# Attention: two rows of one PSUM tile take mask, maxima and exponentials as a pair; reciprocals copied ahead of the lower part; a second bank for the late gates

## The chip, the core and the metric

The kernel runs on one core of one Trainium2 chip. The metric is the device time of one execution in microseconds (us). Each kernel is timed in several runs, and the median is compared. The profile is of one more execution, taken by the hardware profiler.

## What is computed

The reference is one block of a hybrid model, on 1024 tokens of width 1024, in float32: a projection of the normed input, an attention branch with forget gates (8 heads of 64), a recurrent branch (8 heads), sigmoid gates that merge the two, and a convolutional feed-forward part. The change concerns the attention branch and the gates:

```python
logits = einsum('bhqd,bhkd->bhqk', q[q0:q1], k[:q1]) * scale + cum[q] - cum[k]
logits = where(causal, logits, -inf)
probs  = softmax(logits, axis=-1)
o      = einsum('bhqk,bhkd->bhqd', probs, v[:q1])
...
gate_fox, gate_rwkv = split(sigmoid(p_gate), 2)
merged = gate_fox * (o_fox @ fox_w_out) + gate_rwkv * (o_rwkv @ rwkv_w_out)
```

## The kernel before

Matrix products are made in three passes of float32r: each operand is split into a high part (a rounding copy on ACT, named `..._hi`, `th`) and a low part (a subtraction on DVE, `..._lo`, `tl`), and hi*hi + hi*lo + lo*hi are added up in PSUM.

**Stages.** First the input projections with the recurrent branch beside them, then the attention stage, then the branch stage (`br`, the products with `w_br`, multiplied by the gates into `mg`), then the output projection and the feed-forward part. The change lies in the attention stage.

**The attention stage.** For each of 8 heads the queries are cut into 8 rows of 128 (i = 0 to 7), taken in pairs I = 3, 0, 2, 1 (for the last head 0, 1, 3, 2). Three chains are interleaved:

- `s_chain` makes the logits of a row in PSUM (`lg`): 128 x 128(i+1). There are two such tiles of two banks each. A row with i > 3 has a tile to itself; rows 0 and 1 share one, and so do rows 2 and 3, each in its own bank. Then `softmax` is started (L1144): DVE adds the causal mask to the last 128 columns (L1146) and takes the negated maximum `nm` (L1147), ACT makes the exponential `P` with its row sum (L1156). After the exponential of the last row in it, the PSUM tile is free for other logits.
- `t_chain` turns P by transposes on TensorE into a PSUM tile `tp`; `halve` (L1213) splits it: ACT copies `th` (L1215), DVE subtracts `tl` (L1220). At the end of each half of the queries (rows 4 to 7, then 0 to 3) of the heads 0 to 6 the reciprocals of four row sums are transposed into the same tile `tp`, and `spread` (L1172) copies them out (`rt`, on ACT, L1175), stores them to DRAM (`d_rs`, L1177) and loads them back spread over the partitions (`R`, L1181), both by ACT's DMA queue. `rt` has one buffer.
- `a_chain` multiplies th and tl with the values into `ov` (half of a PSUM bank); `collect` copies it out, and POOL multiplies by R.

**What sets the order.** PE, DVE and ACT run in the order in which the program is written here. A small planner, `Weave`, writes it: each chain yields the time at which it is next due, by a cost that the code states for each operation (`weave.use("DVE", ..., 310 + 1.04 * n)`); where no chain is due, it fills TensorE with matmuls of the next projection. In the attention stage the fill is the last 7 gate projections, as 14 halves of 24 matmuls (`late_gate`, L1280), all into one PSUM bank `rk_ps`. When a half is done, ACT applies tanh (`gs`, L1295), and only then can the next half write the bank; `weave.hold` tells the planner for how long it may not fill. What is left of the fill behind the last `ov` runs before the branch stage. The order after that stage's start on ACT, DVE, POOL and SP is set by the compiler's scheduler.

## Time and profile before

| | us |
|---|---|
| median of 3 runs | 1659.14 (1657.43 to 1660.03) |
| the profiled execution, its own time | 1663.44 |
| its span, first to last instruction | 1661.7 |
| TensorE busy in it | 1621.0 (98%) |
| the granted TensorE clock, mean | 0.991 |
| first logits, last `ov`, first branch matmul | 619.2, 812.53 (its end), 826.57 |

A profile row of an instruction reads: start, duration, engine, line, operation, output<-input, shapes, and in brackets how long the engine had been idle and what it waited for. `PE` is TensorE, `PEld` its weight load, `SPq` and `ACTq` are DMA issues. Times in these rows are us from the start of the span.

### The profile page before, as it was taken

What the parts mean: (1) busy time and instruction counts of PE and PEld (TensorE: products, weight loads), DVE (VectorE), ACT (ScalarE), POOL (GpSimd) and SP (SyncE); (2) the same over time, 40 slices, a digit from 0 to 9 for tenths busy, and PEclk for the clock granted to TensorE, in tenths of its full rate; (3) what the DMA queues carried; (4) which work ended last, traced back from release to release, by engine and by line L of the source; (5) the groups of instructions that cost most, each with busy time, mean ns of one, the idle gap of its engine ahead of it and who ended that gap; (6) DMA issues with size and microseconds to landing.
All of it is one profiled execution on the core that took longest, in us unless ns stands there. A gap on an engine that the chain in (4) does not pass through costs nothing.

```text
span 1661.7 us, 25960 instructions
## 1 busy us (share of the span) xinstructions
PE 1621.0 (98%) x9756; PEld 1329.5 (80%) x9756; DVE 1202.9 (72%) x2350; ACT 809.2 (49%) x1473; POOL 136.6 (8%) x169
## 2 busy tenths in 40 slices
PE   7999999999999998999999999999999999999998
PEld 5777877887877777887788888888888888888886
DVE  6875877887886536866579445897777777786677
ACT  7663434443446556665513144654444444555455
POOL 0010101211101020222022000000000000000000
PEclk8999999999999999999999999999999999999999
DMA  9587644443433246542487310243223223574463
GB/s 347 191 308 221 159 131 127 131 125 91 116 101 87 92 156 136 152 119 84 143 284 270 146 73 36 70 138 104 95 96 120 96 95 108 202 272 153 127 209 108
DMA packets 123902, 241.72 MB, mean 145 GB/s; under 512 B 39816, under 2 KB 48320, under 8 KB 123776
## 3 DMA queue, kind: packets, MB, share of 16 engines
q1 hardware_dynamic: 114944, 220.94, 41.1%
q0 software_dynamic: 7600, 17.25, 3.8%
q10 hardware_dynamic: 1232, 1.86, 0.4%
q8 instruction: 77, 1.26, 0.3%
q14 instruction: 49, 0.40, 0.1%
HBM read 174.43 MB, written 65.56 MB: 144 GB/s over the span
## 4 chain that ended last, share of the span: by engine, by line
PE 82%; DVE 8%; ACT 4%; DMA 3%; issue 2%; SPq 0%; POOL 0%; ACTq 0%; DVEq 0%; POOLq 0%
PE X L144 13%; PE D L144 13%; PE Y L144 6%; PE gt L144 6%; PE ps_rkv L144 5%; PE wo L144 5%; PE br L144 5%; PE W L144 3%; PE rk_ps L144 3%; PE qk L144 3%; PE v L144 3%; PE low L144 1%; PE lg L144 1%; PE ov L144 1%; PE sp L144 1%
## 5 line engine op out<-in xcount | busy, mean ns | idle before, releaser
L144 PE MATMUL D<-op,op 128*128 128x512 f32 x924 | 209.8, 390 | 0.0
L144 PEld LDWEIGHTS D<-op,op 128*128 128x128 f32 x924 | 173.4, 188 | 36.2 <-DVE op L1372 0.3
L144 PE MATMUL X<-T_m,S 128*128 128x512 f32 x440 | 107.3, 390 | 0.1
L144 PEld LDWEIGHTS X<-T_m,S 128*128 128x128 f32 x440 | 82.5, 188 | 18.2 <-ACT T_m L1797 0.6
L1371 ACT CAST op<-g 128x512 fp32r<-128x512 f32 x77 | 47.8, 621 | 72.1 <-PE D L144 48.2
L1372 DVE TENSOR_TENSOR op<-g,op 128x512 fp32r<-128x512 f32 x77 | 53.0, 689 | 40.9 <-ACT op L1371 40.8
L1608 DVE SCALAR_TENSOR_TENSOR c<-ab,vec,c 128x512 f32<-128x512 f32 x88 | 65.9, 750 | 19.5 <-ACT c L1611 17.9
L1220 DVE TENSOR_TENSOR tl<-tp,th 128x512 fp32r<-128x512 f32 (+1 forms) x80 | 50.3, 633 | 29.0 <-ACT th L1215 28.4
L1572 DVE TENSOR_TENSOR S<-ur,S 128x512 fp32r<-128x512 f32 x66 | 45.5, 691 | 35.6 <-ACT S L1568 35.4
L270 DVE TENSOR_TENSOR lo_in<-raw_in,hi_in 128x512 fp32r<-128x512 f32 x84 | 58.0, 729 | 16.4 <-PE gt L144 7.5
L1568 ACT CAST S<-ur 128x512 fp32r<-128x512 f32 x66 | 41.0, 622 | 55.6 <-DVE ur L1561 30.6
L1572 DVE TENSOR_TENSOR A<-ur,A 128x512 fp32r<-128x512 f32 x64 | 44.1, 689 | 30.9 <-ACT A L1568 30.7
L266 ACT CAST hi_in<-raw_in 128x1024 fp32r<-128x1024 f32 x42 | 43.9, 1048 | 46.1 <-PE ps_rkv L144 26.2
L795 DVE TENSOR_TENSOR t<-E,M 128x60 f32<-128x60 f32 (+24 forms) x248 | 55.0, 222 | 11.9 <-DMA M<-sm 5.9
L144 PE MATMUL Y<-T_h,A 128*128 128x512 f32 x264 | 63.5, 390 | 0.0
L144 PE MATMUL Y<-T_h,S 128*128 128x512 f32 x264 | 63.3, 390 | 0.0
L799 DVE TENSOR_TENSOR E<-E,t 128x60 f32<-128x60 f32 (+24 forms) x248 | 56.9, 230 | 5.8
L144 PE MATMUL X<-B_b,A 128*128 128x512 f32 x252 | 60.8, 390 | 0.0
L144 PE MATMUL W<-B_f,A 128*128 128x512 f32 x252 | 60.6, 390 | 0.0
L1156 ACT ACTIVATE P<-lg,nm 128x896 f32<-128x896 f32 (+3 forms) x64 | 47.4, 743 | 24.4 <-DVE nm L1147 21.2
L144 PEld LDWEIGHTS Y<-T_h,A 128*128 128x128 f32 x264 | 49.6, 188 | 10.3
L144 PEld LDWEIGHTS Y<-T_h,S 128*128 128x128 f32 x264 | 49.6, 188 | 10.3
(493 smaller groups left out, 4076.9 us busy)
## 6 DMA issues: line engine op xcount, KB each, us to landing
raw_in<-in_w_in SPq DMA_DIRECT2D x50, 512.0 KB
wm<-in_w_mod SPq DMA_DIRECT2D x48, 512.0 KB
ur<-in_w_up SPq DMA_DIRECT2D x44, 512.0 KB
g<-d_g SPq DMA_DIRECT2D x35, 512.0 KB
d_g<-gs SPq DMA_DIRECT2D x44, 256.0 KB
d_g<-c SPq DMA_DIRECT2D x33, 256.0 KB
d_st<-qh SPq DMA_DIRECT2D x64, 128.0 KB
d_gate<-gs SPq DMA_DIRECT2D x32, 256.0 KB
```

The lines of the kernel that those rows point to most:

```text
L144: weave.last = nc.tensor.matmul(o, lhsT, rhs, start=start, stop=stop, skip_group_check=more)
L266: i = nc.scalar.copy(hi, raw)
L270: nc.vector.tensor_tensor(lo[:, c : c + NH], raw[:, c : c + NH], f32(hi[:, c : c + NH]), op=ALU.subtract)
L795: i = tt(tv, E32[:, 0:J, s : s + 1].to_broadcast([128, J, W]), M32[:, s : s + 1, s + 1 : 32].to_broadcast([128, J, W]), op=ALU.mult)
L799: tt(E32[:, 0:J, s + 1 : 32], E32[:, 0:J, s + 1 : 32], tv, op=ALU.add)
L1156: nc.scalar.activation(e[:, 0:n], lg[:, 0:n], AF.Exp, bias=nm[:, 0:1], accum_out=total)
L1220: tt(tl[:, 0:w], tp[:, 0:w], f32(th[:, 0:w]), op=ALU.subtract)
L1371: nc.scalar.copy(hi, src)
L1372: tt(lo, src, f32(hi), op=ALU.subtract)
L1568: nc.scalar.copy(hi, src)
L1572: tt(lo, src, f32(hi), op=ALU.subtract)
L1608: stt(c, ab[:, x + hf * NH : x + hf * NH + NH], V("conv_w", 22 * x + i), c, op0=ALU.mult, op1=ALU.add)
```

## The change

`softmax` now takes a tuple of rows. The two rows that share a PSUM tile are started together when the second one's logits are issued: one mask over both blocks, two maxima, then two exponentials one behind the other. In the last head the scaling of P goes to a function of its own, `scaled`. In `halve` the copy of the reciprocals is issued right behind `th`, ahead of `tl`; its DMA is due 300 ns later by the planner's clock. A late gate that begins when `weave.late` is 2 (behind the attention chains) would take the bank of `ov` in turn with `rk_ps`.

```diff
@@ -1110,7 +1110,8 @@
         seq = [(h, I) for h in range(8) for I in ((0, 1, 3, 2) if h == 7 else (3, 0, 2, 1))]
         lg_free, tp_free, pl_free, ps_free, th_free, ov_free = (deque([0.0] * n) for n in (2, 2, 4, 2, 3, 1))
         probs, av_queue, halves, sums, norms, inverse, landed = {}, deque(), {}, {}, {}, {}, set()
-        ov_ps = pb.tile([128, NH], F32, tag="big", name="ov")[:, 0:256]
+        ov_bank = pb.tile([128, NH], F32, tag="big", name="ov")
+        ov_ps = ov_bank[:, 0:256]
         rk_ps = pb.tile([128, NH], F32, tag="big", name="rk_ps")
 
         def slot(free):
@@ -1138,42 +1139,64 @@
                         c1 = min(n, c0 + NH)
                         mm(lg[:, c0:c1], qa[:, qs], ka[:, c0:c1], start=True, stop=False)
                         mm(lg[:, c0:c1], qb[0:68, qs], kb[0:68, c0:c1], start=False, stop=True)
-                    weave.spawn(softmax(h, i, n, lg), 351)
+                    if i > 3:
+                        weave.spawn(softmax(h, (i,), lgt), 351)
+                    elif i % 2:
+                        weave.spawn(softmax(h, (i - 1, i), lgt), 351)
                     yield 0
 
-        def softmax(h, i, n, lg):
-            nm = at.tile([128, 3], F32, tag="nm", name=f"nm{h}_{i}", bufs=4)
-            tt(lg[:, n - 128 : n], lg[:, n - 128 : n], f32(tri_r), op=ALU.add)
-            nc.vector.tensor_reduce(nm[:, 0:1], lg[:, 0:n], axis=AX.X, op=ALU.max, negate=True)
-            yield weave.use("DVE", weave.now, 310 + 1.04 * n) + 140 - weave.now
-            e = (at.tile([128, S], F32, tag="P", name=f"P{h}_{i}", bufs=4) if i > 3 else
-                 at.tile([128, NH], F32, tag="Ps", name=f"P{h}_{i}", bufs=2))
-            p, hf = h // 2, i // 4
-            if (h, hf) not in sums:
-                sums[h, hf] = at.tile([128, 8], F32, tag="sums", name=f"sums{h}_{hf}", bufs=4), []
-            sm, done = sums[h, hf]
-            total = nm[:, 1:2] if h == 7 else sm[:, i % 4 : i % 4 + 1]
-            nc.scalar.activation(e[:, 0:n], lg[:, 0:n], AF.Exp, bias=nm[:, 0:1], accum_out=total)
-            t = weave.use("ACT", weave.now, 250 + 0.83 * n)
-            if i > 3 or i % 2:
-                lg_free.append(t + 210)
-            if h == 7:
-                yield t + 140 - weave.now
-                nc.vector.reciprocal(nm[:, 2:3], total)
-                ts(e[:, 0:n], e[:, 0:n], nm[:, 2:3], None, op0=ALU.mult)
-                t = weave.use("DVE", weave.now, 230 + 0.53 * n)
-            probs[h, i] = t + 210, e
-            done.append(i)
+        def softmax(h, rows, lgt):
+            hf, k = rows[0] // 4, len(rows)
+            d = rows[0] * 128
+            if k == 1:
+                tt(lgt[:, d : d + 128], lgt[:, d : d + 128], f32(tri_r), op=ALU.add)
+            else:
+                m = lgt[:, d : d + 768].rearrange("p (a c) -> p a c", c=128)[:, ::5, :]
+                tt(m, m, f32(tri_r).unsqueeze(1).to_broadcast([128, 2, 128]), op=ALU.add)
+            t = weave.use("DVE", weave.now, 190 + 130 * k)
+            part = []
+            for i in rows:
+                n = (i + 1) * 128
+                nm = at.tile([128, 3], F32, tag="nm", name=f"nm{h}_{i}", bufs=4)
+                lg = lgt[:, i % 2 * NH :] if k > 1 else lgt
+                nc.vector.tensor_reduce(nm[:, 0:1], lg[:, 0:n], axis=AX.X, op=ALU.max, negate=True)
+                t = weave.use("DVE", weave.now, 120 + 1.04 * n)
+                part.append((i, n, nm, lg))
+            yield t + 140 - weave.now
+            for i, n, nm, lg in part:
+                e = (at.tile([128, S], F32, tag="P", name=f"P{h}_{i}", bufs=4) if i > 3 else
+                     at.tile([128, NH], F32, tag="Ps", name=f"P{h}_{i}", bufs=2))
+                if (h, hf) not in sums:
+                    sums[h, hf] = at.tile([128, 8], F32, tag="sums", name=f"sums{h}_{hf}", bufs=4), []
+                sm, done = sums[h, hf]
+                total = nm[:, 1:2] if h == 7 else sm[:, i % 4 : i % 4 + 1]
+                nc.scalar.activation(e[:, 0:n], lg[:, 0:n], AF.Exp, bias=nm[:, 0:1], accum_out=total)
+                t = weave.use("ACT", weave.now, 250 + 0.83 * n)
+                if i > 3 or i % 2:
+                    lg_free.append(t + 210)
+                if h == 7:
+                    weave.spawn(scaled(h, i, n, nm, e, total), t + 140 - weave.now)
+                else:
+                    probs[h, i] = t + 210, e
+                done.append(i)
...
+        def scaled(h, i, n, nm, e, total):
+            nc.vector.reciprocal(nm[:, 2:3], total)
+            ts(e[:, 0:n], e[:, 0:n], nm[:, 2:3], None, op0=ALU.mult)
+            probs[h, i] = weave.use("DVE", weave.now, 230 + 0.53 * n) + 210, e
+            return
+            yield
+
         def spread(h, hf, tp):
             p = h // 2
             rt = at.tile([4, 128], F32, tag="rt", name=f"rt{h}_{hf}", bufs=1)
             nc.scalar.copy(rt, tp[0:4, 384:512])
-            t = weave.use("ACT", weave.now, 200)
+            t = weave.use("ACT", weave.now, 260)
+            yield t + 300 - weave.now
             nc.scalar.dma_start(d_rs[h, hf * NH : hf * NH + NH].rearrange("(i k) -> i k", k=128), rt)
             if h % 2 == 0:
                 norms[p, hf] = at.tile([128, NH], F32, tag="R", name=f"R{p}{hf}", bufs=2)
@@ -1213,10 +1236,13 @@
         def halve(h, I, jj, tp, w, last):
             th = at.tile([128, NH], F32R, tag="th", name=f"th{h}_{I}{jj}", bufs=3)
             nc.scalar.copy(th[:, 0:w], tp[:, 0:w])
-            yield weave.use("ACT", weave.now, 60 + 0.83 * w) + 140 - weave.now
+            t = weave.use("ACT", weave.now, 60 + 0.83 * w)
+            if last:
+                s_ = spread(h, I // 2, tp)
+                weave.spawn(s_, next(s_))
+                t += 260
+            yield t + 140 - weave.now
             tl = at.tile([128, NH], F32R, tag="tl", name=f"tl{h}_{I}{jj}", bufs=3)
-            if last:
-                weave.spawn(spread(h, I // 2, tp), 0)
             tt(tl[:, 0:w], tp[:, 0:w], f32(th[:, 0:w]), op=ALU.subtract)
             t = weave.use("DVE", weave.now, 70 + 1.04 * w)
             tp_free.append(t + 210)
@@ -1283,17 +1309,22 @@
                 while w[2:] and w[2] not in split:
                     weave.hold = weave.now + 200
                     yield
-                yield from gemm_steps(rk_ps, w[0:2], u, cs)
-                weave.hold = weave.now + 700
+                banks.rotate(weave.late == 2)
+                ps = banks[0]
+                yield from gemm_steps(ps, w[0:2], u, cs)
+                weave.hold = weave.now + 700 if weave.late == 1 else 0.0
                 pending.append((i, hf))
-                weave.spawn(gate_out(i, hf, cs), 260)
+                weave.spawn(gate_out(i, hf, cs, ps), 260)
                 yield
 
-        def gate_out(i, hf, cs):
+        banks = deque([rk_ps, ov_bank])
+
+        def gate_out(i, hf, cs, ps):
 
             g = gsp.tile([128, NH], F32, tag="sp0", name=f"gs{i}_{hf}")
-            nc.scalar.activation(g, rk_ps, AF.Tanh, scale=0.5)
-            weave.hold = weave.use("ACT", weave.now, 480) + 210
+            nc.scalar.activation(g, ps, AF.Tanh, scale=0.5)
+            t = weave.use("ACT", weave.now, 480) + 210
+            weave.hold = t if weave.late == 1 else 0.0
             marks["gate"] = nc.scalar.activation(g, g, AF.Identity, scale=0.5, bias=epsr[:, 3:4])
             weave.use("ACT", weave.now, 480)
             nc.sync.dma_start(d_gate[i, :, cs], g)
```

Three places show how the order moves. The first is on ACT, in the second head, where the reciprocals of rows 0 to 3 of the head before it (`rt_0`, from the tile `tp_11`) are copied. Before, with what each instruction waits for:

```order
L1215 CAST th_11_7235<-tp_11_7226 128x384 [waits PE_49]
L1181 DMA R_7202<-d_rs 64x512 [waits DMAHW4_49]
L1156 ACTIVATE P_0_7272,sums_0_7273<-lg_0_7237,nm_0_7250 128x128 [waits DVE_49]
L1215 CAST th_30_7275<-tp_30_7256 128x512 [waits PE_49]
L1175 COPY rt_0_7277<-tp_11_7226 4x128 [waits DVE_49]
L1177 DMA d_rs<-rt_0_7277 4x128 [waits Activation_49]
L1156 ACTIVATE P_1_7283,sums_0_7273<-lg_0_7237,nm_1_7253 128x256
L1156 ACTIVATE P_4_7300,sums_1_7178<-lg_4_7245,nm_4_7263 128x640
```

and now:

```order
L1238 CAST th_10_7238<-tp_10_7224 128x512 [waits PE_49]
L1238 CAST th_11_7244<-tp_11_7231 128x384 [waits PE_49]
L1197 COPY rt_0_7246<-tp_11_7231 4x128 [waits DMAHW4_49]
L1204 DMA R_7206<-d_rs 64x512
L1200 DMA d_rs<-rt_0_7246 4x128 [waits DMAHW7_49,Activation_49]
L1173 ACTIVATE P_0_7278,sums_0_7279<-lg_0_7248,nm_0_7257 128x128 [waits DVE_49]
L1173 ACTIVATE P_1_7281,sums_0_7279<-lg_0_7248,nm_1_7259 128x256
L1238 CAST th_30_7299<-tp_30_7290 128x512 [waits PE_49]
L1173 ACTIVATE P_4_7306,sums_1_7193<-lg_4_7261,nm_4_7273 128x640 [waits DVE_49]
```

The copy has moved from behind the next tile's cast (`th_30`) to right behind its own tile's (`th_11`); its wait for DVE is gone, and it waits for a DMA queue (the store of the copy before it). The exponentials P_0 and P_1 follow one another.

The second is on PE, at the end of the attention stage: the last tile of `ov` (rows 4 and 5 of the last head), the gate matmuls (`rk_ps`), and the first branch matmul (`br_00`). Before:

```order
L144 MATMUL ov<-th_22_9119,vh_8515 128x256
L144 MATMUL ov<-th_22_9119,vh_8515 128x128
L144 MATMUL ov<-tl_22_9126,vh_8515 128x128
L144 MATMUL ov<-tl_22_9126,vh_8515 128x256
L144 MATMUL rk_ps<-u_hi,lo_in_8583 128x512 x5
L144 MATMUL rk_ps<-u_hi,hi_in_8921 128x512 x8
L144 MATMUL rk_ps<-u_lo,hi_in_8921 128x512 x8
L144 MATMUL rk_ps<-u_hi,lo_in_8922 128x512 x8
L144 MATMUL rk_ps<-u_hi,hi_in_8921 128x512 x8
L144 MATMUL rk_ps<-u_lo,hi_in_8921 128x512 x8
L144 MATMUL rk_ps<-u_hi,lo_in_8922 128x512 x8
L144 MATMUL br_00_9270<-fx_6889,hi_br_9223 128x512
```

and now:

```order
L144 MATMUL ov<-th_21_9124,vh_8537 128x256
L144 MATMUL ov<-tl_21_9133,vh_8537 128x256
L144 MATMUL ov<-th_21_9124,vh_8537 128x256
L144 MATMUL ov<-tl_21_9133,vh_8537 128x256
L144 MATMUL ov<-th_22_9139,vh_8537 128x256
L144 MATMUL ov<-th_22_9139,vh_8537 128x128
L144 MATMUL ov<-tl_22_9147,vh_8537 128x128
L144 MATMUL ov<-tl_22_9147,vh_8537 128x256
L144 MATMUL rk_ps<-u_hi,hi_in_8805 128x512 x8
L144 MATMUL rk_ps<-u_lo,hi_in_8805 128x512 x8
L144 MATMUL rk_ps<-u_hi,lo_in_8806 128x512 x8
L144 MATMUL br_00_9254<-fx_6889,hi_br_9207 128x512
```

Before, the end of one half (5 matmuls) and two whole halves stood behind the last `ov`; now one half does, and the change from the half before it has eight `ov` matmuls between. The destination is `rk_ps` in all of them. The whole stage has 336 gate matmuls in both kernels, 53 of them behind the last `ov` before and 24 now.

The third is on ACT at the start of the branch stage: casts of the branch weights (`hi_br`) and of the recurrent branch's output (`rk_m`), around the last tanh. Before:

```order
L1295 ACTIVATE gs_1_9201<-rk_ps 128x512 [waits DMAHW6_49,PE_49]
L1297 ACTIVATE gs_1_9201<-gs_1_9201,epsr 128x512 [waits Activation_49]
L205 ACT_TABLE_LOAD
L1413 CAST rk_m_9255<-rk_raw_9342 128x512 [waits DMAHW3_49]
L1413 CAST rk_m_9255<-rk_raw_9342 128x512
L1413 CAST rk_m_9259<-rk_raw_9390 128x512 [waits DMAHW5_49,DMAHW1_49]
L1413 CAST rk_m_9259<-rk_raw_9390 128x512
L1413 CAST rk_m_9256<-rk_raw_9438 128x512 [waits DMAHW7_49]
L1413 CAST rk_m_9256<-rk_raw_9438 128x512
L1413 CAST rk_m_9260<-rk_raw_9487 128x512 [waits DMAHW0_49]
L1413 CAST rk_m_9260<-rk_raw_9487 128x512
L1344 CAST hi_br_9300<-raw_br_9298 128x512 [waits DMAHW4_49,PE_49,Pool_49]
```

and now:

```order
L1325 ACTIVATE gs_1_9185<-rk_ps 128x512 [waits DMAHW6_49,PE_49]
L1328 ACTIVATE gs_1_9185<-gs_1_9185,epsr 128x512 [waits Activation_49]
L205 ACT_TABLE_LOAD
L1375 CAST hi_br_9284<-raw_br_9282 128x512 [waits DMAHW5_49,PE_49,Pool_49]
L1375 CAST hi_br_9332<-raw_br_9290 128x512 [waits DMAHW7_49,PE_49,Pool_49]
L1444 CAST rk_m_9239<-rk_raw_9326 128x512 [waits DMAHW4_49]
L1444 CAST rk_m_9239<-rk_raw_9326 128x512
L1444 CAST rk_m_9243<-rk_raw_9374 128x512 [waits DMAHW6_49]
```

The third and fourth cast of branch weights stood behind the eight `rk_m` casts and now stand ahead of them.

## The prediction

> **What bounds the kernel now.** I read the page first, then the busy time by stretch, then the list of waits, then single places.
>
> ```profile
> PE 1621.0 (98%) x9756; PEld 1329.5 (80%) x9756; DVE 1202.9 (72%) x2350; ACT 809.2 (49%) x1473; POOL 136.6 (8%) x169
> ```
>
> TensorE is the bound, and its matmuls stay the same in number and shape. So the change can only win idle time of TensorE, or time in which its clock is cut. It touches the attention stage and the gate projections that fill it, from 619 us (first logits) to 827 us (first branch matmul). The stretches (columns: length, then busy time of PE, weight load, DVE, ACT, POOL, granted clock, DMA share, GB/s) give its idle time:
>
> ```profile
> 813.00:827.00 14.00, 12.63 (x54) 9.77 (x54) 3.12 (x4) 4.58 (x8) 2.53 (x2) 1.00 0.75 264
> sum 208.00, PE 191.66 PEld 163.48 DVE 143.56 ACT 127.17 POOL 37.65; mean PE 31.94 PEld 27.25 DVE 23.93 ACT 21.19 POOL 6.27
> ```
>
> 208.00 - 191.66 = 16.3 us idle. That is what can be won here, besides the clock. DVE (144 of 208) and ACT (127) are not full: they make TensorE wait by order and delay. The list of waits for the same stretch (total, times, longest):
>
> ```profile
> ACT rt L1175 <- DVE tl L1220: 14.6, 12, 1.9
> ...
> PE rk_ps L144 <- ACT gs L1295: 7.2, 7, 2.0
> PE lg L144 <- ACT P L1156: 6.5, 9, 2.0
> ...
> ACT rt L1175 <- DMA d_rs<-rt: 2.0, 1, 2.0
> ```
>
> 7.2 + 6.5 = 13.7 of the 16.3 us: a gate half that waits for the tanh that empties rk_ps, and logits that wait for the exponential that empties their PSUM tile. Both are ACT's work, and ACT itself stood still 14.6 us behind the little copy `rt`.
>
> **Term A: reciprocals copied ahead of the lower part.** Four gaps of TensorE in order of time, then the `rt` copies just ahead of them:
>
> ```profile
> 652.26 0.50 PE L144 MATMUL lg<-stA 128*128 128x512 f32 x1 [1.95 <-ACT P L1156]
> ...
> 739.55 0.79 PE L144 MATMUL rk_ps<-u_hi,hi_in 128*128 128x512 f32 x1 [1.64 <-ACT gs L1295]
> ...
> 758.11 0.50 PE L144 MATMUL lg<-stA 128*128 128x512 f32 x1 [0.41 <-ACT P L1156]
> ...
> 764.39 0.50 PE L144 MATMUL lg<-stA 128*128 128x512 f32 x1 [1.51 <-ACT P L1156]
> ```
>
> ```profile
> 651.06 0.26 ACT L1175 COPY rt<-tp 4x128 f32<-4x128 f32 x1 [1.20 <-DVE tl L1220]
> ...
> 736.94 0.26 ACT L1175 COPY rt<-tp 4x128 f32<-4x128 f32 x1 [1.70 <-DVE tl L1220]
> ...
> 756.27 0.25 ACT L1175 COPY rt<-tp 4x128 f32<-4x128 f32 x1 [1.91 <-DVE tl L1220]
> ...
> 762.71 0.26 ACT L1175 COPY rt<-tp 4x128 f32<-4x128 f32 x1 [1.64 <-DVE tl L1220]
> ```
>
> Each gap (1.95 + 1.64 + 0.41 + 1.51 = 5.5 us) ends on an exponential or tanh queued on ACT behind such a copy, and each copy had waited about as long (1.20 to 1.91) for the lower part `tl` of its own tile. In the changed order the copy stands right behind `th` and has lost that wait (first pair of order pieces above); its DMA to d_rs is issued an instruction or two later, so ACT no longer stands for the copy's end either. What is late next: in five of seven heads the second copy waits for the first one's store to land, which cost 2.0 us once (row above). I leave 1.0 us of the 5.5: **A = -4.5** (bounds -5.5 and, if DMA takes the place, -2).
>
> The new wait: `tl` now stands behind `rt`, 14 times. No row of before shows it; it can cost DVE the copy (0.25) and a semaphore, some 0.3 us each, 4.2 us in all, or nothing. Behind that `tl` DVE has masks and maxima queued; its matmuls (`ov`) have other work ahead. Taken **+0.5**. The later d_rs store and the reload of R delay only POOL's scaling, which nothing needs before the branch stage; at nothing.
>
> **Term B: where the gate halves meet.** Four gaps more:
>
> ```profile
> 791.15 1.66 PE L144 MATMUL rk_ps<-u_hi,hi_in 128*128 128x512 f32 x6 [2.00 <-ACT gs L1295]
> ...
> 802.60 0.73 PE L144 MATMUL rk_ps<-u_hi,hi_in 128*128 128x512 f32 x2 [0.69 <-ACT gs L1295]
> ...
> 814.38 0.98 PE L144 MATMUL rk_ps<-u_hi,hi_in 128*128 128x512 f32 x3 [0.69 <-ACT gs L1295]
> ...
> 820.84 0.96 PE L144 MATMUL rk_ps<-u_hi,hi_in 128*128 128x512 f32 x3 [0.69 <-ACT gs L1295]
> ```
>
> At these last four changes from one half (24 matmuls) to the next nothing else stands on TensorE between them, so tanh is paid in full: 2.00 + 3 x 0.69 = 4.1 us. In the changed order every such change has at least a row of logits or eight `ov` matmuls between (second pair of order pieces: one of them). The second bank does nothing: no matmul from u writes ov, and the last half writes rk_ps as before. That part of the change is dead here, at zero. It is the longer planned softmax that moves the fill: 24 instead of 53 gate matmuls are left behind the last `ov`. Eight `ov` take about 1 us, one row of logits less than tanh with its wait, so I leave 1.2: **B = -2.9** (bounds -4.1 and -1).
>
> **Term C: the clock.** Stretches of 3.4 us laid on the two drops (seventh figure: granted clock):
>
> ```profile
> 650.10:653.50 3.40, 1.45 (x9) 1.15 (x9) 2.28 (x5) 1.59 (x5) 0.00 (x0) 1.00 0.25 66
> 653.50:656.90 3.40, 3.40 (x15) 2.91 (x14) 2.54 (x5) 1.90 (x4) 0.00 (x0) 0.56 0.33 128
> ...
> 735.40:738.80 3.40, 2.31 (x16) 1.89 (x16) 3.10 (x8) 0.99 (x4) 0.59 (x1) 1.00 0.17 61
> 738.80:742.20 3.40, 2.65 (x7) 2.06 (x8) 1.81 (x3) 3.37 (x9) 0.00 (x0) 0.57 0.88 265
> ...
> 790.00:793.40 3.40, 2.25 (x10) 1.75 (x11) 2.27 (x6) 3.32 (x8) 0.00 (x0) 1.00 0.20 75
> ```
>
> After a stretch with 1.45 or 2.31 us of matmuls the next ran at 0.56 and 0.57: 3.40 x 0.44 = 1.5 us lost, 3.40 x 0.43 = 1.5 less some 0.4 where it was idle anyway, 2.6 in all. The gaps in them are the first two of term A, so **C = -2.6** (bounds -2.6 and 0).
>
> The Trainium skill ("TensorE: Matmul & The Clock Gate", "Why this matters for your kernels") says that the clock falls back after about a whole idle window, and advises to keep gaps under some 3 us. By that rule no gap here (2.00 at most) could have cut it, and the sum would be without C. The rows disagree, with a cut behind 1.95 us of idleness; the rule is a rival below.
>
> **Term D: the pair.** Rows by tile, then one pair of rows 2 and 3:
>
> ```profile
> L1146 DVE TENSOR_TENSOR lg<-lg,cst x64: 287/299/300, 620.2 to 800.7; 128x128 f32<-128x128 f32 x64
> L1147 DVE TENSOR_REDUCE nm<-lg x64: 291/758/1225, 620.5 to 801.0; 128x1 f32<-128x896 f32 x8, 128x1 f32<-128x1024 f32 x8, 128x1 f32<-128x128 f32 x8, 128x1 f32<-128x256 f32 x8
> ```
>
> ```profile
> L1253 DVE TENSOR_TENSOR o<-o,ov x32: 416/420/424, 636.7 to 813.0; 64x256 f32<-64x256 f32 x32
> ```
>
> ```profile
> 702.10 0.56 DVE L1147 TENSOR_REDUCE nm<-lg 128x1 f32<-128x384 f32 x1
> ...
> 703.36 0.69 DVE L1147 TENSOR_REDUCE nm<-lg 128x1 f32<-128x512 f32 x1
> ...
> 704.09 0.58 ACT L1156 ACTIVATE P<-lg,nm 128x384 f32<-128x384 f32 x1 [2.48 <-DVE nm L1147]
> ...
> 705.66 0.69 ACT L1156 ACTIVATE P<-lg,nm 128x512 f32<-128x512 f32 x1
> ```
>
> A mask over 2 x 128 elements lies between the 256-wide `o` (0.42) and two masks (0.60); I take 0.42, so DVE saves 16 x 0.18 = 2.9 us of busy time, off the path. From the second row's matmul to its maximum there was a mask and a reduction; now there is the double mask and both reductions: 0.12 + 0.56 = 0.68 more for rows 2 and 3, 0.12 + 0.29 = 0.41 for rows 0 and 1, 0.55 on average. If all of it showed, 16 x 0.55 = 8.8 us. Against it, the second exponential now follows the first at once: above it began 1.57 after a first of 0.58, so up to 1.0 comes back, 0.3 more than the 0.68 lost, and the bounds are +8.8 and -5. Nearest is that the planner books the longer time and lays gate matmuls there, as it has 29 more inside: **+0.5**.
>
> A rule against the pair: the Trainium skill ("PSUM — Partial Sum Buffer", "PSUM bank collisions raise a hardware error") keeps two engines apart only within a bank, and the two rows lie in different banks. By it the first exponential could have run 0.69 us earlier beside the second row's maximum, and pairing would give that up. The trace says that it did not: it began at 704.09, after the second maximum ended at 704.05, although its own ended at 702.66.
>
> **Term E: the handover to the branch stage.**
>
> ```profile
> 820.84 5.74 PE rk_ps L144 x24
> 826.57 13.60 PE br L144 x60
> ```
>
> ```profile
> 812.09 0.44 PE L144 MATMUL ov<-tl,vh 128*128 128x128 f32 x2
> ```
>
> ```profile
> 815.62 0.69 DVE L1275 TENSOR_TENSOR fx<-o,fx 128x512 fp32r<-128x512 f32 x1 [2.24 <-ACT fx L1273]
> ...
> 816.19 2.53 POOL L1345 TENSOR_TENSOR lo_br<-raw_br,hi_br 128x512 fp32r<-128x512 f32 x2 [27.17 <-ACT hi_br L1344]
> ...
> 823.67 0.75 DVE L1391 TENSOR_SCALAR acc<-wm,sc 128x1024 f32<-128x1024 f32 x1 [7.35 <-DMA wm<-in_w_mod]
> 825.44 1.28 DVE L1393 SCALAR_TENSOR_TENSOR acc<-wm,sc,acc 128x1024 f32<-128x1024 f32 x1 [1.02 <-DMA wm<-in_w_mod]
> ...
> 832.75 3.23 ACT L1413 CAST rk_m<-rk_raw 128x512 fp32r<-128x512 f32 x6 [2.33 <-DMA d_gate<-gs]
> ...
> 835.88 1.37 ACT L1344 CAST hi_br<-raw_br 128x512 fp32r<-128x512 f32 x2
> ```
>
> The branch began 14.0 us after the last `ov` (812.53); with one half left it begins about 6 after. Its operands took 3.8 (fx, 816.31) and 4.9 (first lo_br, half of 2.53): ready. The first product mg_m stands on DVE behind two accumulations done at +14.2 and is wanted by the fifth part, four banks on: 6 + 48 x 0.227 = +16.9: covered by 2 us. The third hi_br, wanted then too, stood on ACT behind casts that waited until +20.2; the changed order puts it ahead of them (third pair of order pieces). So no stall, but the loads have 8 us less: **+1.0** (bounds 0 and the handover rival's +5.7).
>
> **Sum.** -4.5 + 0.5 - 2.9 - 2.6 + 0.5 + 1.0 = **-8.0 us**. The profiled execution took 1663.44 (span 1661.7 and 1.7 around it), giving 1655.4; it was 4.3 above the median of the runs, 1659.14. The same -8.0 on the median: **1651.1**.
>
> **The rivals.**
> - *Clock cuts stay.* By the page's rule the cuts have another cause, and C is 0: -5.4, 1653.7. For it: the gap of 2.00 us that ended at 791.15 cut nothing (last row of term C, clock 1.00), though it may have fallen across two stretches. Chance 0.14.
> - *Handover.* If the third hi_br gets its load only when all queued loads are in (+20.2), TensorE waits 20.2 + 0.7 - 16.9 = 4.0 us, and a clock cut follows (1.7): -8.0 - 1.0 + 5.7 = -3.3, 1655.8. For it: DMA share 0.75 there; against: the changed order. Chance 0.13.
> - *The gaps only move.* ACT's strict order makes other logits late; A and B give a third, C nothing: -2.5 + 2.0 = -0.5, 1658.6. Chance 0.14.
> - *Slower: the pair shows.* At the logits' PSUM tile the later exponentials are not covered: +8.8 instead of +0.5, and the idleness keeps the clock cuts: -4.5 + 0.5 - 2.9 + 8.8 + 1.0 = +2.9, and with one more cut (1.7) +4.6: 1663.7. It decides from about 0.5 us shown for each of the 16 pairs (-5.9 + 1.7 + 16 x 0.47 = +3.3). Against it: the first exponential waited for the second row already. Chance 0.09.
> - The forecast: 0.50.
>
> **How the numbers follow.** What a measurement can tell is 0.2%, 3.3 us: faster is below 1655.8. Forecast, clock rival, most of the handover and a little of the moved gaps: 0.75 faster; 0.16 the same; 0.09 slower. The low end takes A and B in full, C, 2 us of the remaining 6.7 of idleness (16.3 - 5.5 - 4.1) and D and E at nothing: -14.2, so 1645. The high end leaves out the slower rival and the worse half of the moved gaps: 1658.5.
>
> **What would show it.** Right: no wait of `rt` for `tl`; TensorE idle between first logits and first branch matmul near 8 us; no half-clock stretch there; 24 gate matmuls behind the last `ov`, and no wait in the first five branch parts. Wrong: waits of `lg` for P above 6.5 us in all, or branch matmuls that wait for hi_br or DVE.

## The result and the profile after

The changed kernel took 1644.36 us (median of six runs, 1639.68 to 1646.90), the kernel before 1660.92 in the runs beside it (1657.43 to 1663.38). The ratio is 0.9888, with a 95% interval of 0.9873 to 0.9903: faster by 18.6 us by the ratio, 16.6 by the medians. The forecast was 8.0 us less, and 1651.1 (1645.0 to 1658.5): the direction was right, the size was less than half, and the median fell 0.6 us below the range. The profiled execution of the changed kernel took 1646.90 (span 1645.1), 16.5 less than that of before.

Where TensorE's attention stage ends: the chain of work that ended last, last gate half and first branch group (start, length; before they stood at 820.84 and 826.57):

```profile
806.13 5.49 PE rk_ps L144 x24
811.62 87.20 PE br L144 x384
```

14.95 us of the 16.6 by which the span shrank lie ahead of the first branch matmul; logits began within 0.1 us of the same place (619.20 before, 619.11 after). The rest comes later: behind the branch stage the kernel before has two stretches of 3.4 us near half clock, the changed kernel one (third figure from the end: the clock):

```profile
930.00:933.40 3.40, 3.40 (x15) 3.02 (x16) 0.34 (x2) 0.00 (x0) 0.00 (x0) 0.56 0.02 5
933.40:936.80 3.40, 3.40 (x10) 2.63 (x9) 0.00 (x0) 0.00 (x0) 0.00 (x0) 0.50 0.00 0
```

```profile
916.90:920.30 3.40, 3.40 (x11) 2.62 (x10) 0.00 (x0) 0.00 (x0) 0.00 (x0) 0.55 0.02 5
```

This last 1.7 us is luck and not owed to the change. In the twelve kernels profiled below, the part from 850 to 960 us has no such stretch in four (granted clock 1.00), one in six and two in two, and kernels on either side of the change are among those with none.

TensorE's busy time in the stretches from 619 us, in the changed kernel:

```profile
660.00:700.00 40.00, 36.45 (x216) 31.79 (x215) 28.18 (x54) 24.27 (x61) 10.23 (x14) 0.91 0.52 144
...
813.00:827.00 14.00, 14.00 (x63) 11.58 (x63) 8.39 (x12) 6.71 (x12) 2.60 (x2) 1.00 0.99 353
sum 208.00, PE 201.23 PEld 175.97 DVE 147.40 ACT 134.04 POOL 40.92; mean PE 33.54 PEld 29.33 DVE 24.57 ACT 22.34 POOL 6.82
```

Idle time fell from 16.3 to 208.00 - 201.23 = 6.8 us, so idle time gives 9.5 of the 14.95. From 660 to 700 the clock is cut (0.91); the branch stage is full, without a wait. TensorE's waits, then ScalarE's, in the changed kernel (total, times, longest):

```profile
PE lg L144 <- ACT P L1173: 3.9, 4, 3.1
PE rk_ps L144 <- ACT gs L1325: 2.5, 4, 1.2
...
```

```profile
ACT P L1173 <- DVE nm L1162: 7.0, 5, 2.9
...
ACT o L1277 <- POOL fx L1296: 4.7, 1, 4.7
ACT rt L1197 <- DMA d_rs<-rt: 1.4, 1, 1.4
```

The wait of `rt` for `tl` (14.6 us) is gone. One wait is new, `o` behind GpSimd's fx, and one of TensorE's gaps is now 3.1 us long.

**Where the other 5.4 us were.** The same stage by the waits of the weight loads (PEld). First the kernel before:

```profile
PEld rk_ps L144 <- ACT gs L1295: 9.9, 8, 2.4
PEld lg L144 <- ACT P L1156: 9.7, 11, 2.4
PEld tp L151 <- issue: 1.6, 4, 0.6
PEld ov L144 <- DVE tl L1220: 1.2, 3, 0.5
PEld lg L144 <- DVE nm L1147: 1.0, 2, 0.5
PEld ov L144 <- DVE o L1253: 0.9, 2, 0.5
PEld tp L151 <- PE ov L144: 0.8, 1, 0.8
PEld tp L151 <- DVE tl L1220: 0.6, 2, 0.3
PEld tp L151 <- DVE P L1163: 0.2, 1, 0.2
```

and the changed kernel:

```profile
PEld lg L144 <- ACT P L1173: 6.0, 5, 3.5
PEld rk_ps L144 <- ACT gs L1325: 3.4, 4, 1.4
PEld tp L151 <- DVE P L1189: 0.6, 1, 0.6
PEld ov L144 <- DVE o L1279: 0.2, 1, 0.2
PEld tp L151 <- issue: 0.2, 1, 0.2
```

25.9 us before and 10.4 after: 15.5 less, where matmul idleness shows 9.5 less. How one gap looks in the two ways, in the kernel before: the matmul's row, then its weight load's.

```profile
812.83 0.86 PE L144 MATMUL rk_ps<-u_hi,lo_in 128*128 128x512 f32 x3
814.38 1.45 PE L144 MATMUL rk_ps<-u_hi,hi_in 128*128 128x512 f32 x5 [0.69 <-ACT gs L1295]
```

```profile
812.83 0.42 PEld L144 LDWEIGHTS rk_ps<-u_hi,lo_in 128*128 128x128 f32 x2
814.37 1.24 PEld L144 LDWEIGHTS rk_ps<-u_hi,hi_in 128*128 128x128 f32 x6 [1.12 <-ACT gs L1295]
```

The gap is 0.69 by the matmuls, whose records run on to 813.69, and 1.12 by the loads, which had stopped at 813.25. The experiments say which of the two counts.

### The profile page after: what moved, and what is told of

The parts are those of the page before. It is cut to its first block, busy times and chain, and to the rows that moved or that the text cites. A ratio compares the mean times of both kernels' runs of the same rounds, so it can differ in the third digit from the quotient of the medians.

```text
span 1645.1 us, 25963 instructions
## 1 busy us (share of the span) xinstructions
PE 1614.0 (98%) x9756; PEld 1327.9 (81%) x9756; DVE 1197.2 (73%) x2334; ACT 808.4 (49%) x1473; POOL 139.7 (8%) x169
## 4 chain that ended last, share of the span: by engine, by line
PE 88%; DVE 6%; ACT 3%; DMA 1%; issue 1%; POOL 0%; SPq 0%; DVEq 0%; ACTq 0%; POOLq 0%
PE X L144 14%; PE D L144 13%; PE Y L144 6%; PE gt L144 6%; PE ps_rkv L144 6%; PE wo L144 5%; PE br L144 5%; PE rk_ps L144 4%; PE qk L144 4%; PE W L144 3%; PE v L144 3%; PE ov L144 2%; PE lg L144 2%; PE tp L151 2%; PE low L144 1%; PE sp L144 1%
## 5 line engine op out<-in xcount | busy, mean ns | idle before, releaser
L144 PEld LDWEIGHTS X<-T_m,S 128*128 128x128 f32 x440 | 82.4, 188 | 18.2 <-ACT T_m L1828 0.6
L1238 ACT CAST th<-tp 128x512 fp32r<-128x512 f32 (+1 forms) x80 | 42.4, 542 | 33.7 <-PE tp L151 31.3
L144 PEld LDWEIGHTS Y<-T_h,A 128*128 128x128 f32 x264 | 49.5, 188 | 10.4
```

The lines of the kernel that those rows point to most:

```text
L144: weave.last = nc.tensor.matmul(o, lhsT, rhs, start=start, stop=stop, skip_group_check=more)
L1238: nc.scalar.copy(th[:, 0:w], tp[:, 0:w])
```

## The experiments

Two theories stood at the start. *The order*: the pair's longer booking makes the planner lay gate matmuls under the softmax, and that filled TensorE. *ScalarE's wait*: the 14.6 us behind `rt` were the root of the small delays too. Besides, a new stall asked for a cause. Ratios are to the kernel before, from runs on the same chip, and "so many us less" is the ratio times before's median.

**One part alone: the reciprocals.**

```diff
 (the kernel before, with only this of the change)
...
+            if last:
+                s_ = spread(h, I // 2, tp)
+                weave.spawn(s_, next(s_))
+                t += 260
...
```

> The kernel before with one part of the change alone: the reciprocals' copy rt goes ahead of the lower part tl, and the row sums' DMA is issued later. In its instruction order 48 gate matmuls are left behind the last ov (53 before, 24 in the changed kernel). Theory one (TensorE's order: the pair's later booking lays the gate matmuls under the softmax, and that is what removed most of the 25.9 us by which weight loads started late in the attention stage): this part alone takes only the wait of the reciprocals away, 4 gaps or some 5 us, ratio 0.997 (0.995 to 0.999). Theory two (the 14.6 us that ScalarE stood behind rt is the root of the smaller delays as well): some 12 us, ratio 0.993, and the weight loads' delays fall to about 12 us with the gate matmuls left where they were.

Measured: 1649.42, ratio 0.9925 (0.9911 to 0.9939), 12.5 us less. Weight loads waited 16.6 us, 9.3 less than before, and the profiled execution had no clock cut in the stage.

```profile
PEld lg L144 <- ACT P L1156: 6.1, 10, 0.8
PEld rk_ps L144 <- ACT gs L1299: 3.6, 3, 1.4
PEld ov L144 <- DVE tl L1224: 2.3, 2, 2.1
```

**One part alone: the pairs.**

```diff
 (the changed kernel with before's spread and halve)
...
-            if last:
-                s_ = spread(h, I // 2, tp)
-                weave.spawn(s_, next(s_))
...
```

> The changed kernel with the rows taken as pairs, but the reciprocals copied where the kernel before copies them, behind the lower part. In its instruction order 26 gate matmuls are left behind the last ov. Theory one (TensorE's order): most of the gain is kept, about 11 us, ratio 0.993 (0.991 to 0.995); the waits of rt for tl come back as TensorE gaps of some 5 us. Theory two (ScalarE's wait for rt is the root): some 4 us or less, ratio 0.998, and the weight loads' delays stay above 20 us.

Measured: 1651.06, ratio 0.9933 (0.9918 to 0.9949), 11.1 us less; weight loads waited 17.0 us, 8.9 less. So each part alone brings what one theory says of it and the other theory excludes: both hold in part. Together the two would take 9.3 + 8.9 = 18.2 us of delay away, and the change took 15.5. The experiments that follow ask what is missing and why each part is worth so much.

**The new stall: three buffers for `o`.** GpSimd, then ScalarE, then TensorE in the changed kernel (a figure in brackets is the idle time ahead):

```profile
677.53 1.43 POOL L1290 TENSOR_TENSOR o<-o,R 128x256 f32<-128x256 f32 x2 [2.71 <-DMA R<-d_rs]
679.03 0.61 POOL L1293 CAST fx<-o 128x512 fp32r<-128x512 f32 x1
679.58 0.76 POOL L1095 DMA_DIRECT2D stA<-d_st  x1
680.34 1.00 POOL L1097 DMA_DIRECT2D stB<-d_st  x1
681.36 1.87 POOL L1296 TENSOR_TENSOR fx<-o,fx 128x256 fp32r<-128x256 f32 x2
```

```profile
683.26 0.36 ACT L1277 COPY o<-ov 64x256 f32<-64x256 f32 x1 [4.65 <-POOL fx L1296]
...
684.01 0.58 ACT L1173 ACTIVATE P<-lg,nm 128x384 f32<-128x384 f32 x1
```

```profile
685.40 0.79 PE L144 MATMUL lg<-stA 128*128 128x512 f32 x1 [3.06 <-ACT P L1173]
685.39 0.29 PEld L144 LDWEIGHTS lg<-stA 128*128 128x128 f32 x1 [3.48 <-ACT P L1173]
```

GpSimd held a buffer of `o` until 683.23, with two DMA issues (1.76 us) between its own steps; ScalarE's copy into the next `o` waited for it, and the exponentials stood behind that copy.

```diff
-                e = (at.tile([128, S], F32, tag="P", name=f"P{h}_{i}", bufs=4) if i > 3 else
+                e = (at.tile([128, S if i > 5 else 768], F32, tag="P" if i > 5 else "Pq", name=f"P{h}_{i}", bufs=2) if i > 3 else
...
-                halves[p, hf] = at.tile([128, NH], F32, tag="o", name=f"o{p}{hf}"), []
+                halves[p, hf] = at.tile([128, NH], F32, tag="o", name=f"o{p}{hf}", bufs=3), []
```

> The changed kernel with three buffers for the o tile in place of two (the exponentials' tile P is split by width to make room). In the profile of the changed kernel TensorE waited 3.06 us at 685.40 for exponentials that stood on ScalarE behind the copy of o, which waited 4.65 us for GpSimd to be done with a buffer of o; a stretch of 6.8 us at half clock followed. If the two buffers are the cause, both go: 3.06 + 3.4 = 6.5 us against that execution, ratio to the kernel before about 0.986 beside 0.989, with every run near the fast ones of the changed kernel (1640). Rival: ScalarE or VectorE waits for the same late reciprocals one step further on (GpSimd's product waited 2.71 us for their DMA, and its queue holds two DMA issues of 1.76 us), so the gap stays between 2 and 3 us and the ratio at 0.989.

Measured: 1639.95 (1639.44 to 1642.26), ratio 0.9874 (0.9858 to 0.9890). The copy ran 5.2 us earlier (1.1 of it because this execution's stage began earlier), and the gap is gone, with the clock cut behind it:

```profile
678.08 0.37 ACT L1277 COPY o<-ov 64x256 f32<-64x256 f32 x1 [0.63 <-PE ov L144]
```

```profile
PEld rk_ps L144 <- ACT gs L1325: 3.4, 4, 1.4
PEld lg L144 <- ACT P L1173: 2.5, 4, 0.9
```

Weight loads wait 7.1 us in all, 18.8 less than before: the 18.2 of the two parts, nearly. The cause of the stall is shown: the wait for GpSimd is gone from the copy, and the gap with it. The rows of P have four buffers as before, now two of each width, so the split gives ScalarE no more room. The rival, that the wait moves one step on, is out. What the third buffer is worth in timed runs is less certain: the ratio's interval overlaps that of the changed kernel (the profiled spans are 1637.9 and 1645.1).

**Two masks in place of one.**

```diff
-                m = lgt[:, d : d + 768].rearrange("p (a c) -> p a c", c=128)[:, ::5, :]
-                tt(m, m, f32(tri_r).unsqueeze(1).to_broadcast([128, 2, 128]), op=ALU.add)
+                for c0 in (d, d + 640):
+                    tt(lgt[:, c0 : c0 + 128], lgt[:, c0 : c0 + 128], f32(tri_r), op=ALU.add)
```

> The changed kernel with the pair's mask added by two instructions of 128 columns in place of one of 2 x 128; all engines keep their order. Busy time of VectorE rises by 16 x (2 x 0.29 - 0.43) = 2.4 us. Theory: the mask lies beside TensorE's gate matmuls and the time is the same, ratio 0.989 within 0.002. Rival: the pair's softmax sets the pace of the attention stage and the time rises by 2 to 3 us, ratio 0.9905.

Measured: 1642.96, ratio 0.9888 (0.9872 to 0.9905), the changed kernel's own; the rival's 0.9905 is the edge of the interval. Weight loads wait 11.0 us beside 10.4. The merged mask is worth nothing that can be told.

**The copy `rt` early, TensorE's order kept.**

```diff
 (the kernel before; all entries in the planner's clocks as before)
...
             nc.scalar.copy(th[:, 0:w], tp[:, 0:w])
+            if last:
+                early[h, I // 2] = at.tile([4, 128], F32, tag="rt", name=f"rt{h}_{I // 2}", bufs=1)
+                nc.scalar.copy(early[h, I // 2], tp[0:4, 384:512])
...
```

> The kernel before, with the copy rt issued on ScalarE right behind the upper part th (ahead of the lower part tl, as in the changed kernel), but with all entries in the planner's clocks as before: TensorE's and VectorE's order are those of the kernel before, with 53 gate matmuls behind the last ov and eight gate halves that follow one another with nothing between. Theory one (ScalarE's wait by itself): the copy rt alone saved what the first experiment showed, weight loads' delays 25.9 to 16.6, ratio 0.993. Theory two (the planner's new order of TensorE, which the booking of rt sets off, gave most of it): only the four gaps behind rt go, 4 to 5.5 us, the waits for the gates' gs stay near 9.9, the half-clock stretches may stay, ratio 0.997.

Measured: 1654.79, ratio 0.9957 (0.9941 to 0.9974), 7.1 us less. The delays of the weight loads fell by 4.3 to 21.6:

```profile
PEld rk_ps L144 <- ACT gs L1298: 9.3, 7, 2.4
PEld lg L144 <- ACT P L1156: 4.6, 8, 1.4
```

The waits for P halved, those for gs stayed, as the second theory of this expectation has it. This profile's stage had no clock cut either, where that of before lost 3.4 us. The 7.1 us hold some of both: the ten runs differ in their mean clock (last section).

**The new order, `rt` late.**

```diff
 (the first experiment's kernel, same entries in the planner's clocks)
...
             tt(tl[:, 0:w], tp[:, 0:w], f32(th[:, 0:w]), op=ALU.subtract)
+            if last:
+                nc.scalar.copy(late.pop((h, I // 2)), tp[0:4, 384:512])
...
```

> The first experiment's kernel (rt alone) with the same entries in the planner's clocks, so the same order on TensorE and VectorE, but the copy rt issued behind the lower part tl, so that ScalarE waits for VectorE again as in the kernel before (some 15 us in all). Theory one (ScalarE's wait by itself): the time returns to that of the kernel before, ratio 0.999. Theory two (the new order): the gs waits stay at 3.6 us as in the first experiment, and 5 to 6 us come from the new order, ratio 0.996 to 0.997. If both hold in part, this ratio's gain and that of the experiment beside it add up to the first experiment's 12.5 us.

Measured: 1662.84, ratio 1.0000 (0.9986 to 1.0014): nothing. The delays are 27.1 us:

```profile
PEld lg L144 <- ACT P L1156: 15.0, 14, 3.4
PEld rk_ps L144 <- ACT gs L1302: 3.8, 4, 1.4
```

The order does what it was credited with, gs 9.9 to 3.8; but while ScalarE stands behind `rt`, the logits take it all back, 9.7 to 15.0. So the two do not add up. The copy alone takes 4.3 us away, the order alone adds 1.2, both take 9.3. (ScalarE's wait itself is not quite that of before: `rt` waits 18.8 us for `tl` in this order, 14.6 in the old one, so part of what the order gives may be lost to a longer wait.) As far as the first part goes, ScalarE's wait is the root, and the order doubles what its removal is worth.

**Pairs alone, three buffers for `o`.** The edit of the third experiment, on the second's kernel.

> The second experiment's kernel (pairs alone) with three buffers for the o tile; same order on all engines. In the second experiment's profile TensorE waited 2.9 us for exponentials behind the copy of o (4.50 us behind GpSimd's fx), and a stretch at half clock followed (granted clock 0.91 from 660 to 700). Theory (stage length is a constant plus the weight loads' delays plus half of the time at half clock): both go, 3.3 + 3.4 us, so the profiled execution comes to 1653.6 - 6.7 = 1647, ratio 0.9905. Rival: the stall comes from the late reciprocals, which this kernel copies late, and moves to ScalarE's next wait: ratio stays at 0.993.

Measured: 1646.93, ratio 0.9914 (0.9900 to 0.9928), the profiled execution 1645.49; delays 13.6 us, 3.4 less than without the buffer. So the stall at `o` is there without the early reciprocals too. The rival's 0.993 is just outside the interval, the expected 0.9905 inside. One weight load still waited 2.3 us for P, and 1.7 us were lost to a clock cut behind it.

**An early function table.**

```diff
 (the third experiment's kernel, with three o buffers)
...
-        nc.scalar.preload_act_table_set("exp_and_others")
+        warm = at.tile([1, 1], F32, name="warm", bufs=1)
+        nc.scalar.activation(warm, epsr[0:1, 3:4], AF.Tanh)
```

> The kernel with three o buffers, and a 1 x 1 tanh ahead of the attention stage, so that ScalarE loads its function table while it is idle, and not at the first late gate, where TensorE stood idle for 1.18 us behind it in every profile so far. Expected: that gap goes and nothing else, 1.2 us less than with three o buffers alone (about 1638.5), ratio 0.9865. Rival: the first gate half is then bound by its activation anyway (gs 0.60 us behind the last matmul into its bank) and 0.6 us at most is gained, which the runs can't tell.

Measured: 1639.22, ratio 0.9868 (0.9851 to 0.9885), the fastest kernel here. The table's load stands at 614.42, ahead of the stage, instead of 621.67 with three buffers alone:

```profile
614.42 1.28 ACT L1341 ACT_TABLE_LOAD   x1
615.72 0.20 ACT L1341 ACTIVATE warm<-epsr 1x1 f32<-1x1 f32 x1
```

Weight loads wait 5.8 us, 1.3 less (1.2 expected). The runs can't tell that from the third experiment's 1639.95.

**The pair's order without the pair.** The second experiment's kernel, with each row's mask ahead of its own maximum again:

```diff
...
+                tt(lg[:, n - 128 : n], lg[:, n - 128 : n], f32(tri_r), op=ALU.add)
                 nc.vector.tensor_reduce(nm[:, 0:1], lg[:, 0:n], axis=AX.X, op=ALU.max, negate=True)
...
```

> The second experiment's kernel (pairs alone) with the pair's entries in the planner's clocks kept, so TensorE and ScalarE keep their order, but each row with its own mask ahead of its own maximum again (mask, maximum, mask, maximum on VectorE). Theory one (the booking of the pair moves the gate matmuls under the softmax): the time stays that of the second experiment, ratio 0.993 to 0.9935. Theory two (one mask, two maxima and two exponentials in a row are quicker by themselves): the first row's exponential may begin earlier but VectorE is longer by 0.18 us a pair, so half or more of the gain goes, ratio 0.996.

Measured: 1651.27, ratio 0.9945 (0.9928 to 0.9963). The interval holds the 0.996 of the second theory too, so the time alone does not decide; the delays are 17.0 us, as with the pair. On this order the pairing of VectorE's own work adds nothing that can be told. What is left for the gain are the order and the two exponentials in a row, which this kernel has as well.

**The pair without its order.** The kernel before, with the first row's mask, maximum and exponential held back to the second row's place:

```diff
...
+                if i % 2 == 0:
+                    first.append(part[0])
+                    part = []
+                else:
+                    part.insert(0, first.pop())
...
```

> The kernel before with all entries in the planner's clocks as before (TensorE's order of the kernel before, 53 gate matmuls behind the last ov), but for the heads 0 to 6 the two rows of a PSUM tile take one mask, both maxima and both exponentials in a row, at the place of the second row. Theory one (the booking moves the gate matmuls): the pair by itself saves nothing; what the forecast bounded at -5 to +8.8 us for 16 pairs shows as about 0 to +3 for these 14, ratio 1.000 to 1.002, weight loads' delays 26 to 29 us. Theory two (the pair is quicker by itself): 5 us or more, ratio below 0.997.

Measured: 1656.98, ratio 0.9978 (0.9965 to 0.9990), 3.7 us less; delays 22.3, 3.6 less. It lies between the two theories: the pair by itself does save something, a third of what pairs and order bring, and on the order of before it is no cost. The waits for P fell from 9.7 to 7.4 us, those for gs from 9.9 to 8.8.

**The account.** For each profiled execution: the stage's length from first logits to first branch matmul (by its own row, which starts 0.16 us ahead of its place in the chain above), TensorE's idle time in it, W the sum of the weight loads' waits, C the clock's loss (length times one minus the granted clock, summed over forty slices), and what remains.

| kernel | length | idle | W | C | length - idle - C | length - W - C |
|---|---|---|---|---|---|---|
| before | 207.21 | 16.3 | 25.9 | 3.4 | 187.5 | 177.9 |
| changed | 192.35 | 6.8 | 10.4 | 3.4 | 182.2 | 178.6 |
| rt alone | 195.12 | 9.4 | 16.6 | 0.0 | 185.7 | 178.5 |
| pairs alone | 198.73 | 11.2 | 17.0 | 3.4 | 184.1 | 178.4 |
| three o buffers | 186.25 | 3.8 | 7.1 | 0.0 | 182.5 | 179.2 |
| two masks | 191.56 | 6.5 | 11.0 | 1.7 | 183.3 | 178.8 |
| rt early, order kept | 199.16 | 11.9 | 21.6 | 0.0 | 187.2 | 177.6 |
| rt late, new order | 210.22 | 17.7 | 27.1 | 5.1 | 187.4 | 178.0 |
| pairs, three o buffers | 194.30 | 8.4 | 13.6 | 1.7 | 184.2 | 179.0 |
| three o buffers, early table | 185.03 | 2.5 | 5.8 | 0.0 | 182.5 | 179.2 |
| pair's order alone | 195.98 | 11.3 | 17.0 | 0.0 | 184.7 | 179.0 |
| pair alone, order kept | 203.33 | 14.1 | 22.3 | 3.5 | 185.7 | 177.6 |

Two rows of the stage, before and changed (length, busy time of each engine):

```profile
619.20:826.41 207.21, 190.87 (x1134) 162.81 (x1133) 143.25 (x286) 126.78 (x290) 37.65 (x51) 0.98 0.45 126
```

```profile
619.11:811.46 192.35, 185.58 (x1135) 163.01 (x1134) 139.01 (x268) 126.02 (x290) 38.32 (x51) 0.98 0.44 125
```

The same matmuls (1134 and 1135 records) are "busy" for 190.87 us in one and 185.58 in the other, at the same clock loss. Less the weight loads' waits the stage is 177.6 to 179.2 us in all twelve, over a range of W from 5.8 to 27.1; less the idle time it is 182.2 to 187.5, by and large the longer the more waits there are. So a wait counts from the end of the last weight load, and part of it lies under the matmuls' records. The Trainium skill ("Perfetto Trace Analysis", "Tensor Engine Instruction (MATMUL, LD_WEIGHTS)") says that TensorE's end times are estimated and not observed; the twelve profiles agree: before and changed differ by 5.3 us of busy time for the same work.

## Why the prediction was wrong

The step that failed is the first: "208.00 - 191.66 = 16.3 us idle. That is what can be won here, besides the clock." What stood there to be won was 25.9 us, the weight loads' waits, and the change won 15.5 of them. Every later term was sized by the smaller figure, and the sum left 6.7 us of idleness standing, of which even the low end took only 2. The forecast's own sign, idle time near 8 us, came out at 6.8, and the time still fell by twice the forecast: idle rows were the wrong measure.

By the weight loads the miss adds up. Without the clock the sum was -5.4. The eight gaps that A and B priced at 9.6 us of idleness are 12.4 us of delay, 2.8 more (A's four: 2.38 + 1.88 + 0.62 + 1.71; B's four: 2.44 + 1.12 + 1.12 + 1.11). The 2.2 us held back from them were won, and the 2.0 us of costs (new wait, D, E) did not come. The other waits were 13.5 us, and all that is left in the changed kernel is 10.4, 3.1 less. 5.4 + 2.8 + 2.2 + 2.0 + 3.1 = 15.5. By point:

- **A, the reciprocals (-4.5).** Right for the copy by itself: 4.3 us with the order kept, by delays and idle time (4.4) alike. It missed that the same edit shifts the planner's bookings, and that copy and new order together take 9.3. The forecast treated the order as something that B alone changes.
- **The new wait (+0.5).** VectorE did stand for it (the wait of `tl` for `rt` is 3.2 us, four times, in the changed kernel), and no weight load waited for `tl` behind it: nothing.
- **B, the gate halves (-2.9).** Right in this: with other work between them the last changes no longer wait (the changed kernel's last wait for gs ends at 760.82), 24 gate matmuls stand behind the last `ov`, and the second bank is unused. The size was off: the waits for gs fell from 9.9 to 3.4, 6.5 us, and 5.8 of them are the four last changes, which the forecast priced at their idle 0.69 and 2.00. The source was too narrow: it is not only the pair's longer booking that moves the fill. With `rt` alone 48 gate matmuls were still behind the last `ov`, and the waits for gs were 3.6 us.
- **C, the clock (-2.6).** The two named stretches ran at full clock, as forecast, and in the kernel with the copy early and the order kept as well. But in the profiled execution of the changed kernel the new stall brought a cut of its own: 3.4 us lost before, 3.4 after. "Clock cuts stay" came true there, for a reason that it did not give. With three `o` buffers on the changed kernel the stage had none. And perhaps not every run of the changed kernel paid for it: two of the six have a mean clock of 0.995 and 0.996 and took 1639.68 and 1640.31 us, the others 0.991 and 0.992.
- **D, the pair (+0.5).** Wrong in sign, within its bounds: 3.6 us of delay saved on the old order. The lower bound was argued from exponentials in a row, and its side won, though not shown to be for that reason; the merged mask itself is worth nothing that can be told.
- **E, the handover (+1.0).** The branch began 5.5 us after the last `ov` (6 forecast), and no matmul of its first parts waited: 0.
- **What was left standing (6.7 us of idleness).** Other waits than those for P and gs add up to 6.3 us by the weight loads before and 1.0 after. Small waits for `tl`, `nm` and `o` go too when the engines ahead of them run early.

The slower rival (the pair shows) is refuted by the pair alone with its order kept, and "the gaps only move" by the account. What nobody named is the stall at `o`: a buffer that had been free in time became late when ScalarE came earlier. It cost 3.3 us of delay in that profile, and 3.4 more by the clock.

Left open: why the new order is worth 5 us more once `rt` is early (the waits show where, not by which step of the planner), and how much of the pair's own 3.6 us comes from the exponentials in a row.

## What to carry to other kernels

Size what a stage of matmuls can gain by the waits of its weight loads, not by TensorE's idle time, and check it: length less waits less clock loss should be the same for any two versions (it was within 1.6 us in the twelve here). Where a planner sets the order, an edit to one engine's step is two changes, the wait and the new order; build each without the other, since neither has to be worth anything alone. After a gain look for the buffer that is now late: here a third `o` buffer gave 3.3 us of delay and a clock cut back in the profile, though the timed ratios overlap.

## What the runs showed of the hardware

The clock fell behind a gap again. The stretches around the new stall (third figure from the end: granted clock):

```profile
681.38:684.79 3.41, 0.96 (x7) 0.51 (x5) 2.35 (x4) 1.53 (x5) 1.85 (x2) 1.00 0.93 302
684.79:688.20 3.41, 2.80 (x7) 2.23 (x8) 1.93 (x6) 2.05 (x6) 0.00 (x0) 0.55 0.51 124
688.20:691.60 3.40, 3.40 (x16) 3.20 (x15) 0.86 (x1) 0.00 (x0) 0.00 (x0) 0.50 0.68 143
```

TensorE was idle for 3.06 us by its matmuls and then ran 6.8 us at half clock, from about 685.1, though it was busy in the second of the two stretches throughout. The Trainium skill ("TensorE: Matmul & The Clock Gate", "What's actually happening") has the slow clock begin after at least one idle window of about 3.4 us. The cut at 685.1 hardly tells against it, because the same gap is 3.48 us by the weight load. A cut in the kernel before does. In stretches that begin and end with the cut:

```profile
650.50:653.92 3.42, 1.66 (x13) 1.57 (x13) 2.27 (x6) 1.78 (x6) 0.00 (x0) 1.00 0.35 101
653.92:657.33 3.41, 3.41 (x12) 2.82 (x11) 2.52 (x4) 2.14 (x5) 0.00 (x0) 0.50 0.23 91
```

TensorE had run matmuls for 1.66 of the 3.42 us ahead of it, and the gap behind which it fell is 1.95 us by the matmuls and 2.38 by the loads. Nor does it take a gap. The two slow stretches of the kernel before at 930 stand behind 32 matmuls of one column each, with no wait of TensorE there by matmuls or by weight loads:

```profile
927.48 4.15 PE L144 MATMUL mps<-cst,acc 128*128 128x1 f32 x32
```

That matmuls so small do not keep the clock up is an inference from this place. All twelve kernels run them, and in four profiles no cut follows.

The same program does not always have the same clock: the kernel with `rt` early and the order kept took 1650.65 to 1651.97 us in the four runs with a mean granted clock of 0.995 to 0.997, and 1654.53 to 1659.23 in the six with 0.990 to 0.993. These are means over the whole execution; where the cuts lay is known for the profiled one alone. What decides it from run to run was not tried.
